# Moving an adaptation vector from vector, Pool and scalar work to column-tiled matmuls, in a hybrid decoder layer on one Trainium2 core

## The chip, the core and the metric

The program runs on one NeuronCore of one Trainium2 chip. TensorE (PE) does the matmuls, and its loading of the stationary operand is shown apart as PEld. VectorE (DVE), ScalarE (ACT) and GpSimd (POOL) do the elementwise work, and SyncE (SP) issues nearly all DMAs. The metric is the time of one execution on the device in microseconds (us). All data are float32; the large matmuls split each operand into a rounded part (hi) and a rest (lo) and add three products in the faster fp32r form.

## The reference

One decoder layer on x (1024 tokens, 1024 channels), conditioned on a vector c of 1024 numbers. What matters here is the first line: `mod` has 6 x 1024 entries, and each of its six parts shifts, scales or gates the whole layer.

```python
c_act = jax.nn.silu(c)
mod = (c_act @ w_ada[l] + b_ada[l])[:, None, :]          # 1024 x 6144 weights, 25 MB
shift1, scale1, gate1, shift2, scale2, gate2 = jnp.split(mod, 6, axis=-1)
h = rms_norm(x, norm1_w[l]) * (1.0 + scale1) + shift1
proj = h @ w_in[l]                    # split into DeltaNet heads (gq gk gv gz ga gb) and attention (sq sk sv)
...                                   # conv + silu + l2 norm, chunked delta rule; sliding-window attention
x = x + gate1 * (jnp.concatenate([o_g, o_s], axis=-1) @ w_out[l])
h2 = rms_norm(x, norm2_w[l]) * (1.0 + scale2) + shift2
x = x + gate2 * ((jax.nn.silu(h2 @ w_gate[l]) * (h2 @ w_up[l])) @ w_down[l])
```

## The kernel before

Activations lie transposed: channels on the 128 partitions, tokens along the free axis, in two halves of 512 tokens. Channel tile k (0 to 7) of x and of h holds channels 128k to 128k+127. The vector `mod` is kept in `modc`, 128 x 48: column u holds entries 128u to 128u+127. Columns 0 to 7 are shift1, 8 to 15 scale1, 16 to 23 gate1, 24 to 31 shift2, 32 to 39 scale2, 40 to 47 gate2. Each column ("unit" u) needs 512 KB of weights, loaded by one DMA (`load_ada`) into a tile `ada{u}`. These tiles share slots by tags: two slots each for b, c, d and e, and other tiles (halves of x, `kd`, `bv`) use the same slots earlier or later.

In the kernel before, row n of unit u's tile is output channel 128u+n, with 1024 weights. silu(c) is spread over all partitions once (`cb`), and a unit is one product with `cb` and a sum along the row. `mod_col` and `start_col` do this in one DVE instruction (CUSTOM_DVE, 128x1024) and a short read of the accumulator, or in a POOL product and an ACT copy with a sum; a DVE addition puts the bias on.

The program has these stages up to the attention scan:

- Start. The sums of squares of the first half of x go through `rstd`; then, tile by tile, `start_in(k)` makes the scale a (from unit 8+k) and the shift sh (from unit k), and from them the modulated h, hi by ACT and lo by DVE (`start_lo`). As soon as tile k is there, `start_mm` multiplies it with the weights of the first units gk0, gk1, gq0, gq1 and with those of three token blocks of the small unit skv. `JOIN` says after which tile a unit begins. The function `o` fixes the order of DVE, ACT and POOL here.
- Second half: `norm1_gen(1)`, then `modulate1` for the eight tiles of the second half of x.
- Fill: a loop of `ADA_ITER` = 14 rounds. Each round issues six steps (`fill(6)`) of the stream of dense matmuls on PE and works off two of the units 16 to 43.
- Token scalars and pairs: `token_gen` makes decay and beta (matmuls `psg`, then `pst`), and the four head pairs go through statistics (`pst_k`, `pst_q`), scaling (`psr_k`) and products (`psA`), with fills of fixed length between (`VISITS_A`).
- Solve: DVE solves the triangular systems (`soltmp`, `lanes`), while value and query visits and the last four units (44 to 47) run beside it (`VISITS_B`). Then the chunk scan begins, at about 345 us.

PE runs in the order in which the code is written. On DVE, ACT, POOL and SP a scheduler fixes one order per engine when the program is built. Each engine works strictly in its own order.

Of the kernel before, what the change touches and what calls it, by code (L numbers as in the profile page):

```python
# [8 lines left out]
F32 = mybir.dt.float32  # L9
# [3 lines left out]
AF = mybir.ActivationFunctionType  # L13
ALU = mybir.AluOpType
# [3 lines left out]
P = 128  # L18
T = 1024
TH = 512  # L20
D = 1024
KT = D // P
# [5 lines left out]
ADA_TAGS = "bcd" * 5 + "bcde" * 4 + "d"  # L28
ADA_ITER = 14
# [25 lines left out]
def tile_hybrid_layer(  # L55
# [175 lines left out]
    a1 = cp.tile([P, KT], F32, name="a1")  # L231
    a2 = cp.tile([P, KT], F32, name="a2")
    adat = {}

    act.activation(out=c_col, in_=c_col, func=AF.Silu)
    cb = t4("cb")
    ps_c = [sm(f"ps_c{g}") for g in range(2)]
    for i in range(KT):
        pe.transpose(out=ps_c[i // 4][:, i % 4 * P:(i % 4 + 1) * P], in_=bc(c_col[:, i:i + 1], (P, P)), identity=ident)

    def copy_cb():
        for g in range(2):
            act.activation(out=cb[:, half(g)], in_=ps_c[g], func=AF.Copy)

    def load_ada(u, tag=None):
        adat[u] = t4(f"ada{u}", tag=tag)
        done["ada"] = sp.dma_start(out=adat[u], in_=ada[u])

    def mod_col(u, eng=dve, bias=True):

        w = adat.pop(u)
        if eng is dve:
            dve.tensor_tensor_reduce(out=w, in0=w, in1=cb, scale=1.0, scalar=0.0, op0=ALU.mult, op1=ALU.add,
                                     accum_out=modc[:, u:u + 1])
        else:
            eng.tensor_tensor(out=w, in0=w, in1=cb, op=ALU.mult)
            act.activation(out=w, in_=w, func=AF.Copy, accum_out=modc[:, u:u + 1])
        if bias:
            dve.tensor_tensor(out=modc[:, u:u + 1], in0=modc[:, u:u + 1], in1=b_ada[:, u:u + 1], op=ALU.add)

    ada_next = [16]

    def ada_some(n, tag, eng=dve):
        for u in range(ada_next[0], ada_next[0] + n):
            if "kd" in done:
                with tc.issue_after(done["kd"].ins):
                    load_ada(u, tag)
            else:
                load_ada(u, tag)
            mod_col(u, eng)  # L270
        ada_next[0] += n


    def rstd(ps, name):
# [170 lines left out]
    def start_col(u):  # L445
        w = adat.pop(u)
        o(dve, "tensor_tensor_reduce", out=w, in0=w, in1=cb, scale=1.0, scalar=0.0, op0=ALU.mult, op1=ALU.add,
          accum_out=modc[:, u:u + 1])

    def start_split(hi, lo, src):  # L450
        o(act, "activation", out=r(hi), in_=src, func=AF.Copy)
# [25 lines left out]
    for k in range(KT):  # L477
        if k % 2 == 0:
            pair = t4(f"sq{k}_0", (P, 2, TH))
        sqk[k] = pair[:, k % 2]  # L480
        o(act, "activation", out=sqk[k], in_=xs(k, 0), func=AF.Square)
        if k == 5:
            for g in range(2):
                o(act, "activation", out=cb[:, half(g)], in_=ps_c[g], func=AF.Copy)
# [24 lines left out]
    start_col(0)  # L509
    with tc.issue_after(queue[dve].ins):  # L510
        rs = rstd(ps, "n1_0")
    queue[dve] = rstd_done["n1_0"]
# [8 lines left out]

    ps_u = [bank(t, f"ps_{kind}{p}_0") for t, (kind, p) in zip(("u", "sw", "u", "sw"), START)]
    ps_s = [sm(f"ps_skv{i}", i) for i in range(3)]

    def start_mm(u, k):
        if u < 4:
            mm3(ps_u[u], wpart(wg[u], k), h_hl(0)(k), k == 0, k == KT - 1)
        else:
            for i in range(3):
                skv_mm(ps_s[i], i, k)  # L530

    def start_in(k):

        a, sh, x = a1[:, k:k + 1], modc[:, k:k + 1], xs(k, 0)
        hi = h_hl(0)(k)[0]
        if k:
            start_col(k)
            start_lo(k - 1)
        start_col(8 + k)
        o(dve, "scalar_tensor_tensor", out=a, in0=modc[:, 8 + k:9 + k], scalar=n1w[:, k:k + 1],  # L540
          in1=pre1[:, k:k + 1], op0=ALU.mult, op1=ALU.add)
        o(dve, "tensor_tensor", out=sh, in0=sh, in1=b_ada[:, k:k + 1], op=ALU.add)
        if k in START_DVE:
            o(dve, "scalar_tensor_tensor", out=x, in0=x, scalar=a, in1=rows[0], op0=ALU.mult, op1=ALU.mult)
            o(act, "activation", out=r(hi), in_=x, func=AF.Identity, bias=sh)
        else:
            o(act, "activation", out=r(hi), in_=x, func=AF.Identity, scale=a, bias=sh)
            o(act, "activation", out=x, in_=x, func=AF.Identity, scale=a, bias=sh)

    def start_lo(k):  # L550
        hi, lo = h_hl(0)(k)
        x = xs(k, 0)
        if k in START_DVE:
            o(dve, "scalar_tensor_tensor", out=r(lo), in0=x, scalar=modc[:, k:k + 1], in1=hi, op0=ALU.add, op1=ALU.subtract)
        else:
            o(dve, "tensor_tensor", out=r(lo), in0=x, in1=hi, op=ALU.subtract)
# [3 lines left out]
    for k in range(KT + 1):  # L560
        if k < KT:
            if k + 2 < KT:
                for u in LOADS[k + 1]:
                    load_w(u)
                load_pair(k + 2)
            start_in(k)
            for step in POOL_AT[k]:
                if step[0] == "w":
                    start_split(wg[step[1]][0], wg[step[1]][1], w_raw[step[1]])
                elif step[0] == "m":  # L570
                    o(pool, "tensor_tensor", out=xs(step[1], 0), in0=xs(step[1], 0), in1=rows[0], op=ALU.mult)
                else:
                    ks_ = slice(2 * step[1], 2 * step[1] + 2)
                    start_split(wk_hi[:, ks_], wk_lo[:, ks_], wk_raw[:, ks_])
        else:
            start_lo(k - 1)
            n1 = norm1_gen(1, 3)
            next(n1)
            ktok = t4("ktok", (P, NB, P))
            vs = t4("vs", (P, NB, P))  # L580
        if k:
            for u in have:
                start_mm(u, k - 1)
            if k <= 2:
                keep_warm(WARM[2 + k])
# [299 lines left out]
    def fill(n):  # L885
        with tc.high_priority():
            for _ in range(n):
                next(dense, None)

    def val(p):  # L890
        run(value_gen(p))

    for i in range(ADA_ITER):
        fill(VISITS_A[0])
        with tc.issue_after(h_done[0].ins), tc.issue_after(h_done[1].ins):
            ada_some(1, ADA_TAGS[2 * i], pool if i not in ADA_DVE else dve)
            ada_some(1, ADA_TAGS[2 * i + 1])
    next(token)
    p0, p1, p2, p3 = PAIRS
    for n, visit in zip(VISITS_A[1:], (token, token, p2, p0, p2, p0, p2, p1, p0, keys, p1, p3, keys, p1, keys, p3, p3)):  # L900
# [45 lines left out]
    for n, visit in zip(VISITS_B, (v0, v1, v2, v3, q0, q0, q1, q1, q2)):  # L946
        fill(n)
        next(visit)
        if visit is v3:
            for i in range(32 - 2 * ADA_ITER):  # L950
                ada_some(1, "b", pool if i % 4 else dve)
    dve.scalar_tensor_tensor(out=a2, in0=modc[:, 32:40], scalar=1.0, in1=n2w, op0=ALU.add, op1=ALU.mult)


# [699 lines left out]
```

## Time and profile before

| | before |
|---|---|
| median of 3 runs | 1319.22 us (1318.56 to 1321.34) |
| profiled execution, own time | 1316.65 us |
| its span on the core | 1314.9 us |
| PE busy | 1192.7 us (91%) |
| DVE busy | 892.6 us (68%) |
| POOL busy | 629.4 us (48%) |
| ACT busy | 538.8 us (41%) |

The span is the time between the first and the last recorded instruction; the rest of the execution's own time lies around it. The shares are means over all stages, and the stages differ: what is changed lies nearly all in the first 345 us, where DVE is the busiest engine, while from there on PE is nearly always busy. Idle time of an engine costs something only where the end waits for it. Fp32 matmuls other than transposes stand as two records each in the trace.

### The profile page before, as it was taken

How to read it: one execution, taken by the hardware profiler on the slowest of the kernel's cores; microseconds unless marked ns; L12 is line 12 of the kernel's file. 1: busy time of each engine (PE TensorE's matmuls, PEld its weight loads, DVE VectorE, ACT ScalarE, POOL GpSimd, SP SyncE). 2: the span in 40 equal slices, each digit the busy share in tenths (PEclk: the TensorE clock that was granted, in tenths of full speed). 3: DMA queues.
4: the chain of work that ended last, by engine and by line, in shares of the span. 5: the costliest groups of instructions: out<-in, count | busy, mean ns of one | idle time of the engine just before them, and what ended most of it. 6: DMA issues, size and time to landing. Idle time of an engine off the chain costs nothing.

```text
span 1314.9 us, 18979 instructions
## 1 busy us (share of the span) xinstructions
PE 1192.7 (91%) x6710; PEld 974.5 (74%) x6710; DVE 892.6 (68%) x1690; ACT 538.8 (41%) x1028; POOL 629.4 (48%) x453
## 2 busy tenths in 40 slices
PE   6867697896999799997998999999999999999998
PEld 5757576684788678785786788777777888888887
DVE  7999989979724677576646416877876875546430
ACT  4373555422434777434356432222232334544430
POOL 4667344534335444344354455545455545455440
PEclk8899799898999899998899999999999999999999
DMA  8727468485639865366845625556665567775651
GB/s 326 233 85 273 144 132 227 133 229 183 199 126 205 132 113 165 106 218 216 288 157 187 207 95 203 208 200 228 212 212 201 176 217 281 250 252 195 201 168 40
DMA packets 167214, 250.62 MB, mean 191 GB/s; under 512 B 40656, under 2 KB 106448, under 8 KB 165584
## 3 DMA queue, kind: packets, MB, share of 16 engines
q1 hardware_dynamic: 157520, 241.03, 56.6%
q0 software_dynamic: 9600, 8.39, 3.9%
q8 instruction: 53, 0.87, 0.3%
q14 instruction: 41, 0.34, 0.1%
HBM read 182.89 MB, written 66.45 MB: 190 GB/s over the span
## 4 chain that ended last, share of the span: by engine, by line
PE 43%; DVE 16%; DMA 8%; issue 4%; POOL 3%; ACT 3%; SPq 0%; DVEq 0%; ACTq 0%; POOLq 0%
PE ps_P L1359 5%; PE ps_P L1358 5%; PE ps_P L1360 5%; DMA wb<-in_wgate_dram 4%; PE ps_S L1358 2%; PE ps_S L1359 2%; PE ps_S L1360 2%; PE ps_c L1358 2%; PE ps_c L1359 2%; POOL wS L193 2%; PE ps_c L1360 2%; DVE wa L1427 1%; PE ps_gz L212 1%; DMA SD<-sd 1%; DVE soltmp L817 1%
## 5 line engine op out<-in xcount | busy, mean ns | idle before, releaser
L193 POOL TENSOR_TENSOR wP<-rP,wP 128x512 fp32r<-128x512 f32 (+1 forms) x84 | 108.3, 1301 | 105.3 <-ACT wP L192 100.2
L1359 PE MATMUL ps_P<-t,wP 128*128 128x512 f32 x308 | 120.4, 391 | 0.0
L1358 PE MATMUL ps_P<-t,wP 128*128 128x512 f32 x308 | 120.4, 391 | 0.0
L1360 PE MATMUL ps_P<-t,wP 128*128 128x512 f32 x308 | 120.2, 390 | 0.0
L193 POOL TENSOR_TENSOR wS<-wa,wS 128x512 fp32r<-128x512 f32 x44 | 62.8, 1437 | 111.8 <-ACT wS L192 78.9
L1360 PE MATMUL ps_S<-T,wS 128*128 128x512 f32 x264 | 102.8, 390 | 0.3 <-POOL wS L193 0.3
L1359 PE MATMUL ps_S<-T,wS 128*128 128x512 f32 x264 | 102.9, 390 | 0.0
L1358 PE MATMUL ps_S<-T,wS 128*128 128x512 f32 x264 | 102.9, 390 | 0.0
L192 ACT ACTIVATE wP<-rP 128x512 fp32r<-128x512 f32 (+1 forms) x84 | 48.4, 590 | 77.6 <-PE ps_P L1360 49.2
L1358 PE MATMUL ps_c<-B,w 128*128 128x512 f32 x176 | 70.5, 401 | 6.1 <-ACT X L1398 6.1
L1360 PE MATMUL ps_c<-B,w 128*128 128x512 f32 x176 | 69.7, 396 | 0.0
L1359 PE MATMUL ps_c<-B,w 128*128 128x512 f32 x176 | 69.7, 396 | 0.0
L1465 ACT ACTIVATE sg<-sg 128x512 f32<-128x512 f32 x33 | 20.9, 632 | 116.0 <-DVE sg L1461 116.0
L1358 PEld LDWEIGHTS ps_P<-t,wP 128*128 128x128 f32 x308 | 57.9, 188 | 12.6
L1360 PEld LDWEIGHTS ps_P<-t,wP 128*128 128x128 f32 x308 | 57.9, 188 | 12.5
L1359 PEld LDWEIGHTS ps_P<-t,wP 128*128 128x128 f32 x308 | 57.8, 188 | 12.4
L192 ACT ACTIVATE wS<-wa 128x512 fp32r<-128x512 f32 x44 | 26.7, 624 | 94.6 <-DVE wa L1426 71.8
L1424 DVE TENSOR_TENSOR ws<-wb 128x512 f32<-128x512 f32 x22 | 23.1, 1051 | 62.1 <-DMA wb<-in_wgate_dram 54.5
L1360 PEld LDWEIGHTS ps_S<-T,wS 128*128 128x128 f32 x264 | 49.6, 188 | 11.1 <-POOL wS L193 0.7
L212 PE MATMUL ps_o<-mix,w_o 128*128 128x512 f32 x128 | 53.7, 420 | 4.2 <-ACT w_o L192 4.2
L1358 PEld LDWEIGHTS ps_S<-T,wS 128*128 128x128 f32 x264 | 49.6, 188 | 10.5
L1359 PEld LDWEIGHTS ps_S<-T,wS 128*128 128x128 f32 x264 | 49.6, 188 | 10.5
(507 smaller groups left out, 3559.4 us busy)
## 6 DMA issues: line engine op xcount, KB each, us to landing
ada<-in_ada_dram SPq DMA_DIRECT2D x48, 512.0 KB, 4.7
AD<-ops SPq DMA_DIRECT2D x11, 1536.0 KB, 5.0
rP<-SD SPq DMA_DIRECT2D x16, 704.0 KB, 5.7
sd<-in_wdown_dram SPq DMA_DIRECT2D x20, 512.0 KB, 5.3
SD<-sd SPq DMA_DIRECT2D x20, 512.0 KB, 3.9
rP<-in_wdown_dram SPq DMA_DIRECT2D x12, 704.0 KB, 5.3
XD<-X SPq DMA_DIRECT2D x22, 256.0 KB, 3.3
xu<-XD SPq DMA_DIRECT2D x22, 256.0 KB, 3.4
```

The source lines that it names most:

```text
L192: act.activation(out=r(hi), in_=src, func=AF.Copy)
L193: last = eng.tensor_tensor(out=r(lo), in0=src, in1=hi, op=ALU.subtract)
L212: pe.matmul(out, lhsT=r(lhs[0]), rhs=r(rhs[0]), start=first, stop=False)
L817: dve.tensor_tensor(out=tv[g], in0=bc(L[:, i, i + 1:32].unsqueeze(1), (P, i, 31 - i)), in1=bc(L[:, 0:i, i:i + 1], (P, i, 31 - i)), op=ALU. ...
L1358: pe.matmul(ps, lhsT=r(wh), rhs=r(xh), start=first and i == 0, stop=False, **kw)
L1359: pe.matmul(ps, lhsT=r(wh), rhs=r(xl), start=False, stop=False, **kw)
L1360: pe.matmul(ps, lhsT=r(wl), rhs=r(xh), start=False, stop=i == n - 1, **kw)
L1424: dve.tensor_tensor(out=s1, in0=a21, in1=a22, op=ALU.add)
L1427: dve.tensor_tensor(out=a12, in0=a12, in1=a11, op=ALU.subtract)
L1465: act.activation(out=out, in_=out, func=AF.Silu)
```

## The change

The weights of a unit are stored the other way (tile `[p, k, n]`: input channel 128k+p, output channel n), with as many bytes. For each unit PE now does eight matmuls in plain fp32 (`ada_rows`): stationary is column k of silu(c), repeated over 32 columns, moving are the 128x128 weights of k. Matmul k goes to column group k mod 4 of the array and so to PSUM partitions 32g to 32g+31. The four partial sums then lie as rows. ACT copies them to SBUF, and one matmul per unit with `sel` (ones at partitions 0, 32, 64, 96) sums them and turns them into a column (`ada_cols`). A DVE addition adds the bias, for four units at a time in the fill and solve stages (`ada_gen`). The DVE, POOL and ACT instructions of `mod_col` and `start_col` are gone, with `cb` and its eight transposes, and the last two blocks of warm-up transposes. In the start stage the columns of tile k stand on PE behind the products of tile k-1. In the fill stage the rows of a group stand after every second round, its copy and its columns one and two groups later, and four more dense steps run before `token`.

```diff
-    def mod_col(u, eng=dve, bias=True):
-        w = adat.pop(u)
-        if eng is dve:
-            dve.tensor_tensor_reduce(out=w, in0=w, in1=cb, scale=1.0, scalar=0.0, op0=ALU.mult, op1=ALU.add,
-                                     accum_out=modc[:, u:u + 1])
-        else:
-            eng.tensor_tensor(out=w, in0=w, in1=cb, op=ALU.mult)
-            act.activation(out=w, in_=w, func=AF.Copy, accum_out=modc[:, u:u + 1])
...
+    def ada_rows(out, us):
+        for n, u in enumerate(us):
+            w = adat.pop(u)
+            for k in range(KT):
+                g = k % 4
+                pe.matmul(out[32 * g:32 * g + 32, n * P:(n + 1) * P], lhsT=bc(c_col[:, k:k + 1], (P, 32)), rhs=w[:, k],
+                          start=k < 4, stop=k >= 4, tile_position=(0, 32 * g))
+
+    def ada_cols(out, row, n):
+        for i in range(n):
+            pe.matmul(out[:, i:i + 1], lhsT=row[:, i * P:(i + 1) * P], rhs=sel, start=True, stop=True)
...
+    def ada_gen(us, q=None):
+        ps = sm(f"ps_ada{us[0]}", q)
+        ada_rows(ps, us)
+        yield
+        row, n = t2(f"ada_row{us[0]}"), len(us)
+        act.activation(out=row[:, 0:n * P], in_=ps[:, 0:n * P], func=AF.Copy)
+        yield
+        ada_cols(ps, row, n)
+        u = us[0]
+        dve.tensor_tensor(out=modc[:, u:u + n], in0=ps[:, 0:n], in1=b_ada[:, u:u + n], op=ALU.add)
+        yield
...
+            start_rows(k)
+        if k:
+            start_lo(k - 1)
+            for u in have:
+                start_mm(u, k - 1)
+        if k < KT:
+            start_cols(k)
             start_in(k)
...
     for i in range(ADA_ITER):
         fill(VISITS_A[0])
         with tc.issue_after(h_done[0].ins), tc.issue_after(h_done[1].ins):
-            ada_some(1, ADA_TAGS[2 * i], pool if i not in ADA_DVE else dve)
-            ada_some(1, ADA_TAGS[2 * i + 1])
+            ada_load(1, ADA_TAGS[2 * i])
+            ada_load(1, ADA_TAGS[2 * i + 1])
+        if i % 2:
+            for g in gens:
+                next(g, None)
+            gens = [g for g in (gens + [ada_gen(ada_open[-4:])])][-3:]
+            next(gens[-1])
+    for _ in range(2):
+        fill(2)
+        for g in gens:
+            next(g, None)
     next(token)
```

What that does to the order on PE in the start stage, around tile 1: before, the products of tile 1 (units gk0 and gk1) follow straight on those of tile 0, and those of gq0 follow on them.

```order
L212 MATMUL ps_gk0_0_297<-h0_130,w_s0_141 128x512
L213 MATMUL ps_gk0_0_297<-h0_130,w_s0_141 128x512
L214 MATMUL ps_gk0_0_297<-h0_130,w_s0_141 128x512
L212 MATMUL ps_gk1_0_298<-h0_130,w_s1_143 128x512
L213 MATMUL ps_gk1_0_298<-h0_130,w_s1_143 128x512
L214 MATMUL ps_gk1_0_298<-h0_130,w_s1_143 128x512
L212 MATMUL ps_gq0_0_299<-h0_130,w_s2_145 128x512
```

Now the same products (numbers of lines and buffers have shifted) have the rows of tile 2 (units 2 and 10) ahead of them and the columns of tile 2 behind them:

```order
L251 MATMUL ps_ada_296<-ada2_298,sml_99 32x128 x8
L251 MATMUL ps_ada_296<-ada10_300,sml_99 32x128 x8
L212 MATMUL ps_gk0_0_289<-h0_125,w_s0_136 128x512
L213 MATMUL ps_gk0_0_289<-h0_125,w_s0_136 128x512
L214 MATMUL ps_gk0_0_289<-h0_125,w_s0_136 128x512
L212 MATMUL ps_gk1_0_290<-h0_125,w_s1_138 128x512
L213 MATMUL ps_gk1_0_290<-h0_125,w_s1_138 128x512
L214 MATMUL ps_gk1_0_290<-h0_125,w_s1_138 128x512
L257 MATMUL ps_ada_296<-sel_119,ada_row0_318 128x1 x2
L212 MATMUL ps_gq0_0_291<-h0_125,w_s2_140 128x512
```

The columns of tile 2, which everything for tile 2 waits for, now stand behind the products of tile 1.

Second place, PE in the fill stage, in the dense unit gq2 of the first half. Before, it runs without a break:

```order
L213 MATMUL ps_gq2_0_804<-h0_130,w_gq2_641 128x512
L214 MATMUL ps_gq2_0_804<-h0_130,w_gq2_641 128x512
L212 MATMUL ps_gq2_0_804<-h1_131,w_gq2_641 128x512
L213 MATMUL ps_gq2_0_804<-h1_131,w_gq2_641 128x512
L214 MATMUL ps_gq2_0_804<-h1_131,w_gq2_641 128x512
```

Now the first group's rows (units 16 to 19) stand in it, six matmuls from its beginning:

```order
L213 MATMUL ps_gq2_0_920<-h0_125,w_gq2_762 128x512
L214 MATMUL ps_gq2_0_920<-h0_125,w_gq2_762 128x512
L251 MATMUL ps_ada16_931<-ada16_897,sml_99 32x128 x8
L251 MATMUL ps_ada16_931<-ada17_899,sml_99 32x128 x8
L251 MATMUL ps_ada16_931<-ada18_927,sml_99 32x128 x8
L251 MATMUL ps_ada16_931<-ada19_929,sml_99 32x128 x8
L212 MATMUL ps_gq2_0_920<-h1_126,w_gq2_762 128x512
L213 MATMUL ps_gq2_0_920<-h1_126,w_gq2_762 128x512
```

All later PE work stands behind unit 18's rows, and these need the DMA of unit 18. Third place, SP, where these loads stand. Before:

```order
L247 DMA ada20_846<-in_ada_dram 128x1024
L247 DMA ada19_816<-in_ada_dram 128x1024
L204 DMA w_gk0_1r_1107<-in_wmain_dram 128x1024
L204 DMA w_gq0_1r_1154<-in_wmain_dram 128x1024
L204 DMA w_gk1_1r_1202<-in_wmain_dram 128x1024
L247 DMA ada22_874<-in_ada_dram 128x1024
L247 DMA ada18_811<-in_ada_dram 128x1024
```

And now:

```order
L243 DMA ada20_990<-in_ada_dram 128x1024
L243 DMA ada19_929<-in_ada_dram 128x1024
L204 DMA w_gq0_1r_1443<-in_wmain_dram 128x1024
L204 DMA w_gk1_1r_1486<-in_wmain_dram 128x1024
L243 DMA ada22_1013<-in_ada_dram 128x1024
L243 DMA ada23_1015<-in_ada_dram 128x1024
L243 DMA ada18_927<-in_ada_dram 128x1024
```

Unit 18's load stands late on SP in both. It has tag d, and both d slots hold the last four channel tiles of the second half of x until `modulate1` is through with them.

## Rows read from the trace of the kernel before

**Rows 1.** Windows by stage: stretch, then busy us of each engine, granted clock.
```profile
0.00:71.20 71.20, 53.78 (x272) 45.46 (x273) 58.67 (x87) 31.34 (x51) 38.92 (x42) 0.86 0.77 268
...
98.60:159.20 60.60, 41.73 (x213) 36.04 (x213) 60.16 (x113) 26.25 (x53) 35.12 (x14) 0.87 0.64 226
159.20:276.90 117.70, 101.52 (x673) 83.39 (x672) 103.44 (x185) 56.49 (x85) 55.20 (x25) 0.92 0.63 165
276.90:345.00 68.10, 52.34 (x248) 43.07 (x246) 63.46 (x179) 17.50 (x28) 26.94 (x19) 0.90 0.60 178
```

**Rows 2.** Groups by line and shape, DVE, 0 to 345 us: busy us, mean ns.
```profile
L438 DVE CUSTOM_DVE_ANT_0 ada<-ada,cb 128x1024 f32<-128x1024 f32 x16 | 27.2, 1700 | 0.5 <-DMA ada<-in_ada_dram 0.5
L253 DVE CUSTOM_DVE_ANT_0 ada<-ada,cb 128x1024 f32<-128x1024 f32 x15 | 20.4, 1361 | 0.0
...
L259 DVE TENSOR_TENSOR modc<-modc,sml 128x1 f32<-128x1 f32 x32 | 9.6, 314 | 0.1
...
L332 DVE SCALAR_TENSOR_TENSOR h<-xt,modc,h 128x512 fp32r<-128x512 f32 x4 | 7.1, 1786 | 0.0
L330 DVE SCALAR_TENSOR_TENSOR xt<-xt,a,row_n 128x512 f32<-128x512 f32 x4 | 6.5, 1690 | 1.4 <-ACT row_n L288 1.4
...
L438 DVE SCALAR_TENSOR_TENSOR h<-xt,modc,h 128x512 fp32r<-128x512 f32 x4 | 6.0, 1512 | 0.1
```

**Rows 3.** Groups by line and shape, POOL, 0 to 345 us.
```profile
L256 POOL TENSOR_TENSOR ada<-ada,cb 128x1024 f32<-128x1024 f32 x17 | 42.6, 2518 | 29.7 <-DMA ada<-in_ada_dram 13.4 <-DVE soltmp L817 10.4 <-DVE modc L259 5.7
```

**Rows 4.** Timelines of DVE and ACT: start us, us; one tile's h, then the second half.
```profile
57.87 0.82 ACT L438 ACTIVATE h<-xt,modc,a 128x512 fp32r<-128x512 f32 x1 [1.76 <-DVE modc L438]
...
92.61 0.74 DVE L332 SCALAR_TENSOR_TENSOR h<-xt,modc,h 128x512 fp32r<-128x512 f32 x1
...
97.37 1.28 DVE L337 TENSOR_TENSOR h<-xt,h 128x512 fp32r<-128x512 f32 x2
```

**Rows 5.** Timeline of PE: warm-up, end of the start stage, dense matmuls, psg.
```profile
17.73 3.83 PE L304 MATMUL warm<-ident 128*128 128x128 f32 x32
...
71.22 0.95 PE L321 MATMUL ssps<-ones,sq 128*128 128x1 f32 x8
...
104.16 0.39 PE L213 MATMUL ps_gq<-h,w_gq 128*128 128x512 f32 x1
104.38 0.39 PE L214 MATMUL ps_gq<-h,w_gq 128*128 128x512 f32 x1
...
110.00 0.29 PE L214 MATMUL ps_skv<-wk_hi,h 128*128 128x272 f32 x1
110.13 0.29 PE L212 MATMUL ps_skv<-wk_hi,h 128*128 128x272 f32 x1
...
157.73 0.69 PE L666 MATMUL psg<-tsc,tribd 128*128 128x64 f32 x2 [12.11 <-DVE tsc L661]
```

**Rows 6.** Timeline of PE: small and full fp32 matmuls (stationary size, moving size, records).
```profile
197.40 2.59 PE L781 MATMUL psA<-kq,kn 64*64 64x128 f32 x64
...
362.48 1.16 PE L1039 MATMUL pk<-S,kvq 128*128 128x128 f32 x8
363.39 0.48 PE L212 MATMUL ps_gz<-h,w_gz 128*128 128x512 f32 x1
...
388.99 0.68 PE L1054 MATMUL pd<-rvt,kvq 64*64 64x64 f32 x16
389.51 1.09 PE L1064 MATMUL po<-rvt,aqb 64*64 64x64 f32 x16
```

**Rows 7.** DMA issues, 0 to 100 us: count, KB each, us to landing.
```profile
ada<-in_ada_dram SPq DMA_DIRECT2D x25, 512.0 KB, 4.6
```

**Rows 8.** Timeline of DVE and POOL in the solve.
```profile
311.58 5.00 POOL L256 TENSOR_TENSOR ada<-ada,cb 128x1024 f32<-128x1024 f32 x2 [10.41 <-DVE soltmp L817]
...
314.25 2.59 DVE L817 TENSOR_TENSOR soltmp<-lanes 128x238 f32<-128x238 f32 x1
319.06 0.38 DVE L817 TENSOR_TENSOR soltmp<-lanes 128x228 f32<-128x228 f32 x1
```

More of the change, by code (lines that the diff above doesn't have):

```diff
@@ L235, in tile_hybrid_layer, with ada_load @@
     act.activation(out=c_col, in_=c_col, func=AF.Silu)
[L236 to L243, printed above, removed]
+    sel = cp.tile([P, 1], F32, name="sel")
+    pool.memset(sel, 0.0)
+    for g in range(4):
+        pool.memset(sel[32 * g:32 * g + 1], 1.0)
     def load_ada(u, tag=None):
-        adat[u] = t4(f"ada{u}", tag=tag)
+        adat[u] = t4(f"ada{u}", (P, KT, P), tag=tag)
         done["ada"] = sp.dma_start(out=adat[u], in_=ada[u])
-    def mod_col(u, eng=dve, bias=True):
-        w = adat.pop(u)
-        if eng is dve:
-            dve.tensor_tensor_reduce(out=w, in0=w, in1=cb, scale=1.0, scalar=0.0, op0=ALU.mult, op1=ALU.add,
-                                     accum_out=modc[:, u:u + 1])
-        else:
-            eng.tensor_tensor(out=w, in0=w, in1=cb, op=ALU.mult)
-            act.activation(out=w, in_=w, func=AF.Copy, accum_out=modc[:, u:u + 1])
-        if bias:
-            dve.tensor_tensor(out=modc[:, u:u + 1], in0=modc[:, u:u + 1], in1=b_ada[:, u:u + 1], op=ALU.add)
+    def ada_rows(out, us):
[8 more added lines that the diff above has]
+            pe.matmul(out[:, i:i + 1], lhsT=row[:, i * P:(i + 1) * P], rhs=sel, start=True, stop=True)
     ada_next = [16]
-    def ada_some(n, tag, eng=dve):
+    ada_open = []
+    def ada_load(n, tag):
         for u in range(ada_next[0], ada_next[0] + n):
@@ L269, in ada_some @@
                 load_ada(u, tag)
-            mod_col(u, eng)
+            ada_open.append(u)
         ada_next[0] += n
+    def ada_gen(us, q=None):
[9 more added lines that the diff above has]
+        yield
     def rstd(ps, name):
@@ L443, in load_pair, with start_rows, start_cols @@
             load_ada(u, tag)
[L445 to L448, printed above, removed]
+    adarow = {}
+    def start_rows(k):
+        ada_rows(ps_a[:, k % 2 * 256:], (k, k + 8))
+    def start_cols(k):
+        if not k:
+            adarow[0] = t2("ada_row0")
+        row = adarow[0][:, k % 2 * 256:k % 2 * 256 + 256]
+        o(act, "activation", out=row, in_=ps_a[:, k % 2 * 256:k % 2 * 256 + 256], func=AF.Copy)
+        ada_cols(ps_a[:, k % 2 * 256:], row, 2)
     def start_split(hi, lo, src):
@@ L481, in tile_hybrid_layer @@
         o(act, "activation", out=sqk[k], in_=xs(k, 0), func=AF.Square)
-        if k == 5:
-            for g in range(2):
-                o(act, "activation", out=cb[:, half(g)], in_=ps_c[g], func=AF.Copy)
         if k:
@@ L508, in tile_hybrid_layer @@
         pe.matmul(ps[:, i:i + 1], lhsT=sqk[0][:, i * P:(i + 1) * P], rhs=ones1, start=True, stop=True)
-    start_col(0)
     with tc.issue_after(queue[dve].ins):
@@ L523, in tile_hybrid_layer @@
     ps_s = [sm(f"ps_skv{i}", i) for i in range(3)]
+    ps_a = sm("ps_ada", 3)
     def start_mm(u, k):
@@ L535, in start_in @@
         hi = h_hl(0)(k)[0]
[L536 to L540, printed above, removed]
+        pa = ps_a[:, k % 2 * 256:]
+        o(dve, "scalar_tensor_tensor", out=a, in0=pa[:, 1:2], scalar=n1w[:, k:k + 1],
           in1=pre1[:, k:k + 1], op0=ALU.mult, op1=ALU.add)
-        o(dve, "tensor_tensor", out=sh, in0=sh, in1=b_ada[:, k:k + 1], op=ALU.add)
+        o(dve, "tensor_tensor", out=sh, in0=pa[:, 0:1], in1=b_ada[:, k:k + 1], op=ALU.add)
         if k in START_DVE:
@@ L575, in tile_hybrid_layer @@
         else:
-            start_lo(k - 1)
             n1 = norm1_gen(1, 3)
@@ L581, in tile_hybrid_layer @@
         if k:
[L582 to L585, printed above, removed]
             for new in [u for u in range(5) if JOIN[u] == k - 1]:
@@ L891, in val @@
         run(value_gen(p))
+    gens = []
     for i in range(ADA_ITER):
@@ L949, in tile_hybrid_layer @@
         if visit is v3:
-            for i in range(32 - 2 * ADA_ITER):
-                ada_some(1, "b", pool if i % 4 else dve)
+            ada_load(32 - 2 * ADA_ITER, "b")
+            gens = ada_gen(ada_open[-4:], 2)
+        if visit in (q0, q1):
+            next(gens, None)
     dve.scalar_tensor_tensor(out=a2, in0=modc[:, 32:40], scalar=1.0, in1=n2w, op0=ALU.add, op1=ALU.mult)
@@ L1632 @@
         "rowvec": _np.concatenate([f["a_log"][0], f["dt_bias"][0], f["sinks"][0]]),
-        "ada": w_ada.T.reshape(48, P, D),
+        "ada": tiles(w_ada),
         "wmain": tiles(_np.concatenate([w_in[:, 512:1024], w_in[:, 0:512], w_in[:, 1024:2048], w_in[:, 2064:2576]], axis=1)),
```

## Prediction, written before the changed kernel ran

> **What bounds it now.** I read the windows by stage first. In the start stage DVE is busy for 58.7 of 71.2 us and PE for 53.8; in the fill stage (98.6 to 159.2 us) DVE for 60.2 of 60.6 and PE for 41.7; between the token scalars and the last pair product (159.2 to 276.9) DVE for 103.4 of 117.7 and PE for 101.5; in the solve DVE for 63.5 of 68.1 [rows 1]. So DVE leads in each, though in the third stretch PE is close behind. The groups by line then say how much of DVE's time belongs to the vector: 27.2 us of products in the start, 20.4 in fill and solve, and 32 additions with 9.6 us [rows 2]; POOL spends 42.6 us in 17 products [rows 3]. The timeline shows where PE feels it: `psg` waits 12.11 us for DVE's `tsc` and starts at 157.73 [rows 5]. After 345 us PE hardly waits, and a time won or lost earlier shifts the rest.
>
> The removed instructions are thus on the busiest engine. What speaks against a plain gain is that in the start and the fill PE now does the vector itself, in its own strict order, and waits for its DMAs there.
>
> **Price of a unit on PE.** Eight plain fp32 matmuls stand as 16 records with a 128-column moving side. No row of before has 32 stationary columns in four column groups. Two rows bound the price. `psA`, 64x64 in alternating quarters of the array with 128 columns moving: 2.59 us for 64 records, 40 ns each. `pk`, the full array with 128 columns: from 362.48 to 363.39 for 8 records, 114 ns each [rows 6]. I take the former, as only there do neighbours in the program use different parts of the array: 16 x 40 = 0.65 us per unit. At 114 ns it is 1.82 us. The columns of four units are 8 records, priced like the 8 of `ssps`, 0.95 us [rows 5].
>
> One thing speaks against the low price. `psA` alternates in rows and columns of the array; the new matmuls use all rows. `pd` and `po`, both with one half of the rows, stand at 0.68 and 1.09 us for 16 records [rows 6]: `pd` alternates between column halves and `po` does not, so columns alone do overlap. The Trainium skill ("TensorE: Matmul & The Clock Gate", Part 3: Packing small matmuls) says that a weight load overlaps running matmuls only if its row group differs. By that rule the four column groups run one after the other, and the sum would take 1.82 us for a unit in place of 0.65; the `pd` row speaks for overlap.
>
> **(a) Start stage, +7 us (2 to 12).** DVE loses 27.2 us of products. But PE's order now ties tile k to tile k-1: the columns of k stand behind all products of k-1. From these columns to the end of the products of k the chain is: columns of two units 0.48, then `a` and `sh` on DVE 0.3 to 0.6, h on ACT 0.82 and x as long [rows 4], `lo` on DVE 0.74 (by the undisturbed `L332` of the same size [rows 4]), and the products. One dense matmul follows another after 0.22 us and one with 272 columns after 0.13 [rows 5], so 12 and 9 of them take 3.85 us, of which 3.6 lie behind `lo`. That is about 7.0 us per tile, with PE idle for half of it. A walk with these steps from the end of the shortened warm-up (17.73 + 24 x 0.12 = 20.6 [rows 5]) and the units joining as before gives columns at 31.4 (tile 2), 42.7 (tile 4), 52.9 (tile 5), 59.9 and 66.9, and the last product at 73.1, against 71.2 now [rows 1, 5]. This holds no disturbance. h on DVE takes 1512 ns in the mean here [rows 2], about double of 0.74, with POOL splitting weights beside it; that stays, is now inside the chain, and ACT has the second half's loads and copies before some of the h. I add 5 us for it: +7, between the floor of 2 and 12 with twice that.
>
> **(b) Second half, -4 us (-8 to 0).** Here POOL's products are gone. `L332` and `L330` average 1786 and 1690 ns [rows 2] where an undisturbed one takes 0.74 [rows 4]: 8 x 1.0 = 8 us of excess. POOL also has other work, so I take half.
>
> **(c) Fill, `psg` 17.7 us later.** Unit 18's tile has tag d and waits until `modulate1` ends, 98.65 us before (97.37 + 1.28 [rows 4]), then 4.6 us for its DMA [rows 7]. All later PE work stands behind that wait. From there to `psg` PE has, by the order, 144 dense matmuls of 512 columns (x 0.2275 = 32.8), 96 of 272 (x 0.125 = 12.0), 26 units' rows (x 0.65 = 16.9) and seven sets of columns (x 0.95 = 6.7): 68.2 us, and about 1 for the slower clock after the wait. So `psg` starts at 98.6 + 7 - 4 + 4.6 + 68.2 + 1 = 175.4, and not at 157.7. DVE falls to some 40 us of work here and is no longer the bound: of its gain of 20 us nothing can be used. Among these 68.2 us are the rows and columns, 23.6 us, which PE did not have; before, it idled 18.9 us here [rows 1]. That is the crux: work is moved into the one engine that cannot be late afterwards. With 114 ns per record the 26 units take 47.3 in place of 16.9: +30.4. With 32 ns, pd's spacing to `po` (0.52 / 16 [rows 6]), -3.4.
>
> **(d) To the last `psA`, -3 us (-14 to 0).** Four more dense steps (12 matmuls, 2.7 us) and one DVE convolution of about that size now lie ahead of `psg` and no longer in this stretch. No adaptation work lay between 159.2 and 276.9, so DVE's 103.4 us [rows 1] stay otherwise; PE's 101.5 stay less 2.7. The idle 16.2 us of PE could at the most be given back if the later `psg` finds DVE's queue already worked off, hence the far end.
>
> **(e) Solve, -4 us (-7.4 to 0).** `soltmp` takes 2.59 us while POOL runs a product of two (5.00 us) and 0.38 otherwise [rows 8]. Three such cases and one product of 1.36 on DVE [rows 2] make 7.4. Against it stands that the last group's four units share the two slots of tag b, so the third and fourth wait for the first's rows on PE and then for a DMA of 4.6 us [rows 7], with PE standing still: I take 4.
>
> **(f) From the scan on, -2.7 us (-2.7 to 0).** The dense work done earlier is missing here, where PE is the bound.
>
> **Sum.** +17.7 (a, b and c together) - 3 - 4 - 2.7 = +8.0. The profiled execution has 1316.65 us, so 1324.7; the median of the runs shown lies 2.6 above it, and the same offset gives **1327 us**. Edits costed at nothing are the bias additions (one per four units, in DVE's idle time), the ACT copies (ACT is busy for 35 of 61 us at the most in the fill [rows 1]) and the `sel` memsets before the first load has landed.
>
> **Rivals.** What a measurement of this kernel can tell from no change is about 0.2%, 2.6 us.
>
> *Faster, 1315 (chance 0.25).* The place is the stretch behind `psg`. PE's idle 16.2 us there are waits for DVE's statistics and scalings. In the fill DVE now has 20 us of idle time, and by its order takes up what the scheduler puts there: second-half convolutions and the solve's preparation. If 12 us more than I assume are worked off ahead of `psg`, the stretch shrinks by (d)'s far end and the sum is +8.0 - 12 = -4.0, that is 1315 for the median; with (a) at its floor 1310. It decides from about 8 us worked off. For it speaks DVE's 88% share in the stretch; against it, that the pairs' work depends on q and k that PE makes late.
>
> *The column groups run serially, 1362 (0.13).* Then 30.4 us are added in the fill and about 5 in the start (two units' rows, 2.3 us more per tile, partly in PE's idle time): 1327 + 35. The Trainium skill's rule, weighed above, would give this; `pd` against `po` speaks against it.
>
> *The terms cancel, within 2.6 us of 1319 (0.12).* The start at its floor (-5) and the solve at its far end (-3.4) are enough.
>
> **How the numbers follow.** My forecast, slower by 3 to 20 us, has 0.50; serial columns 0.13; faster 0.25; none 0.12. So faster 0.25, same 0.12, slower 0.63. For the range I leave one in ten out on each side: 1310 below (the faster case with little beyond its middle) and 1352 above, which is short of full serial running but holds a price of about 85 ns per record or a start at +12 with more waits for loads. The forecast's own range is 1322 to 1339.
>
> **What the profile after would show.** Rows of four units in 2.6 us of PE (7.3 if serial). The last product of the start near 78 us, with PE idle for 3 us ahead of each tile's first products, released by ACT or DVE. A PE wait for the DMA of unit 18 near 102 to 106, and `psg` near 175 with no wait for DVE. `L332` and `L330` near 1.2 us. DVE half idle in the fill, but as long as before, 100 us or more, between `psg` and the last `psA`, which ends near 290. `soltmp` at 0.4 us throughout, and a PE wait for the DMA of unit 46. Wrong it would be above all if `psg` came at 165 or earlier, or if the stretch behind it took 105 us or less.

## The result, and the profile after

The changed kernel is slower: 1359.51 us in the median of 4 runs (1350.97 to 1361.23) against 1318.89 before, ratio 1.028 [1.023, 1.033]. The forecast was 1327, with a range that ended at 1352. The profiled execution has 1360.69 us, 44.0 more than that of before. Where the lead is lost is read from the PE timelines, at four places that both programs pass:

| start of, us | before | after | later by | forecast |
|---|---|---|---|---|
| `ssps` behind the last product of the start | 71.22 | 84.53 | 13.3 | 7 |
| `psg` | 157.73 | 178.09 | 20.4 | 17.7 |
| last `psA` | 271.94 | 302.48 | 30.5 | 14.7 |
| first `psm` (scan) | 353.85 | 389.49 | 35.6 | 10.7 |
| end of the span | 1314.9 | 1358.7 | 43.8 | 8.0 |

The lines of the last `psA` and the first `psm`, before and after:

```profile
271.94 2.59 PE L781 MATMUL psA<-kq,kn 64*64 64x128 f32 x64
353.85 1.09 PE L997 MATMUL psm<-tx,aqb 32*32 32x32 f32 x32
...
302.48 2.59 PE L797 MATMUL psA<-kq,kn 64*64 64x128 f32 x64 [2.28 <-DVE kq L781]
389.49 1.09 PE L1025 MATMUL psm<-tx,aqb 32*32 32x32 f32 x32
```

The windows by stage of the changed kernel (stretch, its length, busy us of PE, PEld, DVE, ACT and POOL with counts, granted clock, DMA share, GB/s) answer to [rows 1]:

```profile
0.00:84.50 84.50, 64.50 (x544) 54.70 (x545) 27.20 (x55) 33.60 (x53) 32.94 (x47) 0.90 0.67 232
84.50:108.20 23.70, 12.67 (x100) 10.70 (x98) 21.99 (x41) 15.24 (x33) 9.43 (x6) 0.90 0.28 89
108.20:178.10 69.90, 66.92 (x713) 58.54 (x714) 25.31 (x62) 19.78 (x40) 7.18 (x3) 0.94 0.53 189
178.10:305.10 127.00, 100.49 (x664) 82.12 (x662) 102.47 (x180) 58.69 (x86) 53.79 (x24) 0.88 0.57 149
305.10:390.00 84.90, 69.71 (x397) 56.24 (x398) 62.56 (x189) 19.72 (x31) 28.65 (x20) 0.90 0.65 188
```

DVE falls from 58.7 to 27.2 us in the start and to 25.3 of 69.9 in the fill, where PE has 66.9. Behind `psg` DVE has as much to do as before, 102.5 us, in a stretch that grew. The timeline of the changed kernel (start, us, engine; wait in brackets) shows the places at which PE stands:

```profile
56.78 0.50 PE L257 MATMUL ps_ada<-sel,ada_row 128*128 128x1 f32 x4
58.73 0.49 PE L212 MATMUL ps_gk<-h,w_s 128*128 128x512 f32 x1
...
60.42 1.06 ACT L192 ACTIVATE w_gk2h<-w_gk2r 128x1024 fp32r<-128x1024 f32 x1 [1.85 <-DMA w_gk2r<-in_wmain_dram]
61.39 0.80 ACT L451 ACTIVATE xt<-xt,modc,a 128x512 f32<-128x512 f32 x1
...
61.56 2.35 POOL L193 TENSOR_TENSOR w_gk2l<-w_gk2r,w_gk2h 128x1024 fp32r<-128x1024 f32 x1 [4.88 <-ACT w_gk2h L192]
...
62.22 2.23 DVE L451 TENSOR_TENSOR h<-xt,h 128x512 fp32r<-128x512 f32 x1 [4.55 <-ACT xt L451]
...
64.51 0.80 PE L213 MATMUL ps_gk<-h,w_s 128*128 128x512 f32 x1 [5.28 <-DVE h L451]
70.40 0.50 PE L257 MATMUL ps_ada<-sel,ada_row 128*128 128x1 f32 x4
...
98.24 1.08 PE L251 MATMUL ps_ada<-ada,sml 128*32 128x128 f32 x32
111.17 1.94 PE L251 MATMUL ps_ada<-ada,sml 128*32 128x128 f32 x32 [11.86 <-DMA ada<-in_ada_dram]
...
123.21 1.95 PE L251 MATMUL ps_ada<-ada,sml 128*32 128x128 f32 x64
125.09 0.50 PE L212 MATMUL ps_gk<-h,w_gk2h 128*128 128x512 f32 x1
...
178.09 0.33 PE L682 MATMUL psg<-tsc,tribd 128*128 128x64 f32 x2
...
210.85 1.97 PE L741 MATMUL psr_k<-ident,wide_k 128*128 128x128 f32 x8 [8.46 <-ACT wide_k L737]
...
345.72 1.08 PE L251 MATMUL ps_ada<-ada,sml 128*32 128x128 f32 x16 [7.75 <-DMA ada<-in_ada_dram]
```

Four units' rows take 125.09 - 123.21 = 1.88 us for 64 records: 29.4 ns each, 0.47 us a unit. In the start, ACT's split of a weight tile, itself waiting for its load, stands between h and x of one tile, and POOL's half of the split runs into `lo`, so PE waits 5.28 us. In the fill PE waits 11.86 us for unit 18. In the solve it waits for units 44 to 47, 11.4 us in all, and 7.75 us of that for unit 45. The waits of PE up to 390 us (us in total, times, longest):

```profile
PE ps_ada L251 <- DMA ada<-in_ada_dram: 23.3, 5, 11.9
PE psr_k L741 <- ACT wide_k L737: 13.2, 2, 8.5
```

### The profile page after: what moved, and what is told of

Its sections match the earlier page's. It is cut to its first block, busy times and chain, and to the rows that moved or that the text cites. A ratio compares the mean times of both kernels' runs of the same rounds, so it can differ in the third digit from the quotient of the medians.

```text
span 1358.7 us, 20582 instructions
## 1 busy us (share of the span) xinstructions
PE 1234.5 (91%) x7558; PEld 1011.6 (74%) x7558; DVE 817.3 (60%) x1604; ACT 529.0 (39%) x1010; POOL 581.5 (43%) x441
## 4 chain that ended last, share of the span: by engine, by line
PE 54%; DVE 20%; DMA 12%; issue 5%; ACT 4%; POOL 3%; SPq 1%; DVEq 0%; ACTq 0%; POOLq 0%
PE ps_P L1386 5%; PE ps_P L1388 5%; PE ps_P L1387 5%; DMA wb<-in_wgate_dram 3%; PE ps_S L1386 2%; PE ps_S L1388 2%; PE ps_c L1386 2%; PE ps_S L1387 2%; PE ps_c L1387 2%; PE ps_c L1388 2%; DMA SD<-sd 2%; POOL wS L193 2%; DMA sd<-in_wdown_dram 2%; PE ps_ada L251 1%; DVE wa L1455 1%
## 5 line engine op out<-in xcount | busy, mean ns | idle before, releaser
L1452 DVE TENSOR_TENSOR ws<-wb 128x512 f32<-128x512 f32 x22 | 26.4, 1198 | 60.0 <-DMA wb<-in_wgate_dram 55.7
```

The source lines that it names most:

```text
L1452: dve.tensor_tensor(out=s1, in0=a21, in1=a22, op=ALU.add)
```

## The experiments

The theory formed from these rows is one of waits: PE's strict order puts the columns of a tile too late, and units 18 and 45 to 47 are asked for before their slots are free. The rival is one of work: the loss is simply the matmuls that PE did not have before (48 x 0.47 us of rows and some 11 us of columns, about 34 us). All edits are to the changed kernel where nothing else is said.

**First group off tag d.**

```diff
-ADA_TAGS = "bcd" * 5 + "bcde" * 4 + "d"
+ADA_TAGS = "bcbc" + "ddbc" + "bcdd" + "bcde" * 4
```

> Units 16 to 19 take the tags b, c, b, c in place of b, c, d, b, so none of the first group needs a slot that the second half of x still holds; the two d slots go to units 20 and 21. Theory of the waits: the 11.86 us that PE stood before the rows of unit 18 go, psg comes at 167 to 170 in place of 178, and the time falls by 8 to 11 us, to about 1350. Rival, the work itself: the loss is the 34 us of matmuls that PE did not have before, PE has little else to do while it waits, and the time falls by less than 3 us.

Measured: 1.0185 [1.0146, 1.0225] of before. `psg` comes at 169.36 though the start ended 1.5 us later, and the longest wait for a load there is 1.2 us. The ratio fell by about 13 us, a little more than expected. So the wait was paid in full.

**Columns earlier in the start.**

```diff
-            for u in have:
+            for u in have[:1]:
                 start_mm(u, k - 1)
...
             start_cols(k)
             start_in(k)
+        for u in have[1:]:
+            start_mm(u, k - 1)
```

> In the start stage the columns of tile k and its scale, shift and h stand behind the products of tile k-1 with the first unit only, and ahead of those with the other units. Theory of the order: the chain of a tile runs beside three of four or five products, the last product ends at 74 to 78 us in place of 84.5, and the time falls by 6 to 10 us. Rival: the start is held by its loads and by the weight splits on ACT and POOL, the end of the stage moves by less than 3 us and so does the time.

Measured: 1.0176 [1.0143, 1.0208]; the start ends at 76.27, and the ratio fell by about 14 us, more than expected. Later kernels with this start, in the same order on PE, DVE and ACT, ended it at 71.53, 79.86 and 76.06, so it differs by 8 us between executions, more than with the start as it was changed (84.5 to 87.1 in seven profiles). The two ranges do not meet.

**The last four units as two pairs.**

```diff
-            gens = ada_gen(ada_open[-4:], 2)
+            steps = [lambda: ada_rows(ps_l, us[:2]), lambda: ada_rows(ps_l[:, 256:], us[2:]), last_copy, last_cols]
```

> The last four units run as two pairs: the rows of 44 and 45 at the first visit of the first query, those of 46 and 47 sixteen dense steps later, then one copy and the columns. Theory of the waits: of the 11.4 us of waits for these units' loads some 8 stay out, and the time falls by 5 to 9 us. Rival: the chain to wide_s, for which the kernel before waited 13.4 us at the same place, is next; the first psm moves by less than 2 us and so does the time.

Measured: 1.0264 [1.0223, 1.0304]. The waits for units 46 and 47 are gone, but that for unit 45 is not:

```profile
341.00 1.08 PE L251 MATMUL ps_last<-ada,sml 128*32 128x128 f32 x16 [7.29 <-DMA ada<-in_ada_dram]
356.19 1.08 PE L251 MATMUL ps_last<-ada,sml 128*32 128x128 f32 x32
```

The last `psA` to the first `psm` takes 82.3 us in place of 87.0 (81.9 before), so the place is right in part. The wait for unit 45, 6.7 to 8.0 us, stays in every later kernel with two last pairs; no run here removes it. The scan behind it was 12 us longer in this profile, and the time hardly moved, against the 5 to 9 us expected. More on that below.

**Half of the rows.**

```diff
-            for k in range(KT):
+            for k in range(4):
...
-                          start=k < 4, stop=k >= 4, tile_position=(0, 32 * g))
+                          start=True, stop=True, tile_position=(0, 32 * g))
```

> Only the matmuls with the first four of the eight input tiles are done for each unit, one per column group, so each entry is a sum over half of its inputs. All loads, slots, copies, columns and waits stay. Rows take half, about 0.24 us per unit in place of 0.47. If the loss is PE's added work, the time falls by all of it, 11 us. By the theory of the waits only the 26 units behind the wait for unit 18 count, and it falls by 5 to 7 us.

Measured: 1.0232 [1.0183, 1.0282], some 7 us less, though the interval overlaps that of the changed kernel. The trace is clearer: `psg` comes at 170.90, 7.2 earlier, with the start 0.7 us longer. So of PE's work that of the fill is paid, as the theory of the waits has it, and not all 11 us.

**All three edits.**

> The three edits together: first group off tag d, columns of tile k ahead of most products of tile k-1, last four units as two pairs. If the parts add, the start ends at 76 us, psg comes at 159 to 161, the last psA at 281 to 284 and the first psm at 362 to 366 (353.85 in the kernel before), and the ratio to the kernel before is 1.006 to 1.012. Rival: the parts share one cause (whatever PE gains early it waits for later), and the ratio stays above 1.014.

Measured: 1.0135 [1.0109, 1.0161], a little above the expected range and just below the rival's 1.014. `psg` comes at 154.84, 3 us ahead of the kernel before. Then the lead is lost: last `psA` at 277.73, first `psm` at 362.60. So a loss sits behind `psg` that none of the three edits touches.

**Without the extra dense steps.**

```diff
-    for _ in range(2):
-        fill(2)
-        for g in gens:
-            next(g, None)
     next(token)
...
         fill(n)
+        for g in gens:
+            next(g, None)
```

> As the run with all three edits, but without the four extra dense steps ahead of psg: the last two groups' copies and columns go with the first two visits of the token scalars. Theory: the extra steps bring one more convolution to DVE and ACT, which the order puts into the chain from psg to the first scaling, and take four steps of cover from later. Then psg to the last psA falls from some 122 us to 114 to 117, as in the kernel before, and the ratio to before is 1.000 to 1.006. Rival: these stretches are long for another reason; psg comes 3 us earlier, psg to the last psA stays at 121 or more, and the time is that of the run with all three edits.

Measured: 1.0093 [1.0062, 1.0123], above the expected range. `psg` to the first `psr_k` falls from 32.8 to 26.9 us (27.7 before), but to the second from 41.5 only to 40.6 (35.8 before), and `psg` to the last `psA` is 119.5 (122.9 with the steps). Half of the theory held.

**One column group.** All eight matmuls at tile position (0, 0), adding up in one row.

> The changed kernel with all eight matmuls of a unit in column group 0, adding up in one row; only that row is copied and turned. If the four column groups run beside each other, as the 29.5 ns per record say, then one group costs 58 ns (the po row) to 114 ns (the pk row) per record, 0.93 to 1.8 us per unit, and the time rises by 12 to 35 us over the changed kernel. Rival, the rule that loads overlap only across row groups: the four groups did not run beside each other either, the price per unit stays at 0.47 us, and so does the time.

Measured: 1.067 [1.0635, 1.0705], 1408.31 us, 49 more than the changed kernel and above the 12 to 35 expected. The timeline of PE has four units in 7.17 us, 112 ns a record:

```profile
149.88 7.17 PE L250 MATMUL ps_ada<-ada,sml 128*32 128x128 f32 x64
```

So the four column groups do run beside each other, 3.8 times as fast. That one group also adds up in one row is not what makes it slow: the products of `pk` [rows 6] go to columns of their own and take 114 ns.

**The start of before, fill on PE.** Units 0 to 15 as in the kernel before, 16 to 47 on PE, first group off tag d, two last pairs, no extra steps.

> The start stage of the kernel before (its products on DVE, cb, order and warm-up), but units 16 to 47 on PE as in the changed kernel, with the first group off tag d, the last four as two pairs and no extra dense steps. If the loss lies in the start's order, in the waits for unit 18 and for units 45 to 47 and in the extra steps, all four are gone: the start ends at 71 to 73, psg comes at 152 to 155 (157.73 before), and the ratio is 0.995 to 0.999. Rival: PE's added work of the fill is paid in full behind psg, the stretch to the last psA is 121 us or more as in the changed kernel, and the ratio is 1.003 or more.

Measured: 1.0062 [1.0038, 1.0086]; `psg` at 149.10, but 120.4 us to the last `psA` (114.2 before). The ratio is the rival's and the stretch nearly so: of the lead of 8.6 us, 6.2 were given back there. DVE's groups say with what, and it is not PE's work. In the kernel before, DVE did three convolution steps on keys between `psg` and the first `psA`; here and in the changed kernel it does nine, and ACT loads its function tables more often. Groups of the kernel before, 157.7 to 197.4 us (busy us, mean ns):

```profile
L365 DVE SCALAR_TENSOR_TENSOR kn<-ps_gk,sml,kn 128x511 f32<-128x511 f32 (+2 forms) x3 | 2.2, 746 | 2.9 <-ACT kn L363 2.9
...
L379 ACT ACT_TABLE_LOAD x1 | 1.3, 1283 | 3.4 <-DVE kn L371 3.4
```

and of the changed kernel, 178.1 to 223.5 us:

```profile
L378 DVE SCALAR_TENSOR_TENSOR kn<-ps_gk,sml,kn 128x511 f32<-128x511 f32 (+2 forms) x9 | 6.7, 740 | 2.0 <-ACT kn L376 2.0
...
L392 ACT ACT_TABLE_LOAD x3 | 3.8, 1283 | 3.4 <-DVE kn L384 3.3
```

The six more belong to pair 3. Its tile `kn3` is one of six in a pool of 4 KB slots. In the program before, `cb` kept one of the six to the end of the solve, and `kn3` had to wait for pair 2's tile. The change takes `cb` away, `kn3` gets its place at once, and the fixed orders of DVE and ACT now put its convolution ahead of the scalings that PE waits for.

**The slot kept.** A tile like `cb` is read once, when the first values are there:

```diff
+    hold = t4("hold")
+    pool.memset(hold[:, 0:1], 0.0)
...
+    pool.tensor_tensor(out=held, in0=hold[:, 0:1], in1=vts[0][:, 0:1], op=ALU.add)
```

> The changed kernel with one more tile that keeps a slot of the 4 KB pool until the value visits, as cb did in the kernel before. Theory of the freed slot: without cb, pair 3's keys (kn3) get a slot at once, and their nine convolution steps and the ACT table loads stand on DVE and ACT ahead of the scaling of pairs 2 and 0, for which PE waits. With the slot kept, kn3 has to wait for pair 2's tile again, psg to the first psA falls from 45.4 us to 39 to 41, and the time by 4 to 7 us. Rival: the four extra dense steps alone make that stretch long; it stays at 44 or more, and the time within 2 us of the changed kernel.

Measured: `psg` to the first `psA` is 41.1 us (45.4 without), but the time is 1.030 [1.0256, 1.0342], no better, where 4 to 7 us were expected: the scan took 202.4 us in place of 187.6. In the first 41 us DVE now has three key steps and ACT one of these table loads:

```profile
L381 DVE SCALAR_TENSOR_TENSOR kn<-ps_gk,sml,kn 128x511 f32<-128x511 f32 (+2 forms) x3 | 2.2, 742 | 2.0 <-ACT kn L379 2.0
...
L395 ACT ACT_TABLE_LOAD x1 | 1.3, 1283 | 0.0
```

> All three edits, no extra dense steps, and the slot kept. By the theory psg to the first psA falls from 46.0 us to 39 to 41, the first psm comes at 355 to 358 (353.85 before), and the ratio to before is 1.003 to 1.007 (1.0093 without the kept slot). Rival: it is lost again at the next wait, and the ratio stays at 1.009.

Measured: 1.0017 [0.9993, 1.0042]; `psg` to the first `psA` 38.9 us (46.0 without the slot), first `psm` at 351.01, earlier than expected. That is no difference from the kernel before.

> The start of the kernel before, fill and last four units on PE, no extra dense steps, and cb's slot kept until the value visits. By the theory psg comes at 149 again, psg to the first psA takes 39 to 41 us in place of 46.4, and the first psm is at 345 to 348, 6 to 9 us ahead of the kernel before: ratio 0.995 to 1.002. Rival: the stretches behind psg give the lead back whatever kn3 does, and the ratio is that of the same kernel without the kept slot, 1.006.

Measured: 0.9968 [0.9946, 0.999]; 39.1 us (46.4 without), first `psm` at 345.61. So the freed slot is shown as a cause three times. Up to the last `psA` the three pairs agree better still: `psg` to there is 116.9, 112.3 and 112.5 us with the slot kept, 124.4, 119.5 and 120.4 without, so the slot is worth 7.2 to 7.9 us.

**Half of the fill on PE.** As the last, with units 16, 17, 20, 21, ... on PE, 18, 19, 22, 23, ... on DVE, none on POOL.

> As the last one, but in the fill only two of each four units go to PE and two stay on DVE; none goes to POOL. PE then has 14 units' rows and fewer columns less, some 9 us, and DVE 14 products of 1.2 us that POOL no longer disturbs. By the theory of PE as the bound of the fill, psg comes at 140 to 145 and the ratio is 0.990 to 0.997. Rival: with the DVE products back, psg waits for DVE's tsc as in the kernel before, psg stays at 149 or later, and the ratio is 0.998 or more.

Measured: 0.9917 [0.9879, 0.9955], 1312.37 us: faster than both kernels, by 0.8% against the one before. Its windows:

```profile
71.10:95.00 23.90, 20.12 (x129) 16.53 (x128) 22.19 (x43) 16.34 (x33) 11.39 (x6) 0.97 0.39 119
95.00:140.90 45.90, 45.90 (x417) 39.95 (x416) 37.83 (x96) 15.39 (x35) 6.40 (x3) 0.98 0.70 271
140.90:257.90 117.00, 98.73 (x669) 81.29 (x668) 102.19 (x189) 57.04 (x85) 53.92 (x26) 0.91 0.64 165
```

In the fill PE is now busy all of 45.9 us and DVE for 37.8: with the work shared, `psg` comes at 140.91, 10.1 us ahead of the run before it. Of the 17.2 us by which the first `psm` is earlier than in the kernel before (336.62 for 353.85), the time keeps about 11.

**The scan, again.** Gains up to the first `psm` did not always reach the end. Further executions of the kernel before and of two edited ones ask whether the scan behind it is the kernel's or the execution's doing.

> The kernel before, unchanged, profiled again. From the first psm to the last one it took 186.1 us. If the length of the chunk scan is a matter of the clock granted in one execution and not of the kernel, this profile shows another length, between 186 and 202 us, with the same waits. Rival: the scan of the kernel before always takes 186 us, and the edits make it longer.

> As the last one, a further execution: between 186 and 202 us from the first psm to the last by the theory of the execution, 186 again by the rival.

> The changed kernel with the last four units as two pairs, profiled again. Its first profile had 199.7 us from the first psm to the last, at a granted clock of 0.5 to 0.8 in several stretches of 10 us. By the theory of the execution another length, 187 to 202 us, while the first psm stays within 2 us of 381. Rival: the edit itself makes the scan longer, and it takes 198 us or more again.

> The changed kernel with the slot kept, profiled again: first profile 202.4 us from the first psm to the last. By the theory of the execution 187 to 202 us, and psg to the first psA again 41 us. Rival: keeping the slot makes the scan longer, 200 us or more again.

Windows from the first `psm` to the last, of the kernel before in the second of its three profiles:

```profile
353.49:547.90 194.41, 185.42 (x1808) 151.88 (x1808) 108.80 (x429) 110.34 (x296) 78.03 (x82) 0.91 0.64 144
```

of the kernel with the last four units as two pairs:

```profile
382.74:582.50 199.76, 189.75 (x1795) 155.38 (x1794) 102.46 (x430) 110.31 (x296) 76.42 (x81) 0.87 0.61 137
```

and of the changed kernel:

```profile
389.49:577.12 187.63, 177.63 (x1796) 145.64 (x1795) 105.36 (x436) 110.53 (x296) 76.90 (x82) 0.94 0.65 146
```

The kernel before took 186.1, 194.4 and 191.4 us in three profiles, with its first `psm` within 0.5 us each time: 8 us belong to the execution, and the granted clock goes with it (0.98, 0.91, 0.94). That speaks against the rival. But the kernel with two last pairs took 199.6 and 199.8, and that with the kept slot 202.4 and 200.3 (0.87 and 0.88), twice alike. That speaks against the theory, and the kernel with all three edits had 197.7 at 0.88. So within one kernel the lower clock goes with the longer scan; across kernels it does not tell all (187.6 to 193.9 us at 0.94), and what sets it in a kernel stays open. From the first `psm` to the end the kernel before took 961.1, 970.9 and 966.2 us, the changed kernel 969.2.

## Why the prediction was wrong

**What bounds the kernel, (b) and (c)** held. DVE was freed, and the second half fell from 27.4 to 23.7 us (-3.7; forecast -4). Taking half of the excess was right for a reason that the rows show: of the two slow DVE steps, `L330` and `L332` of before (`L343` and `L345` now), only one had POOL's products beside it (two groups of DVE, busy us and mean ns, then the timeline of POOL).

```profile
L343 DVE SCALAR_TENSOR_TENSOR xt<-xt,a,row_n 128x512 f32<-128x512 f32 x4 | 7.0, 1808 | 1.4 <-ACT row_n L301 1.4
...
L345 DVE SCALAR_TENSOR_TENSOR h<-xt,modc,h 128x512 fp32r<-128x512 f32 x4 | 2.9, 737 | 0.0
...
91.45 6.41 POOL L347 TENSOR_TENSOR xt<-xt,row_n 128x512 f32<-128x512 f32 x4 [3.94 <-ACT row_n L301]
```

`L345` fell from 1786 to 737 ns, while `L343` still has POOL's own four tiles beside it and stays at 1808 (1690 before). The fill is PE's: from unit 18 to `psg` 66.9 us, forecast 68.2 and 1 for the clock, which was granted at 0.50 for 4.8 us behind the wait. The load landed 3.0 us behind the last row of `modulate1`, not 4.6. That `psg` came within 3 us of the forecast is partly luck: the start was 6 us longer than forecast, the fill 4 us shorter, and in the fill cheaper units (12.2 us in place of 16.9) made up for other work that was 3.4 us dearer.

**The price of a unit** was taken too high, 0.65 us for 0.47: the alternating column groups need 29.4 ns per record, near the 32 of `pd` and not the 40 of `psA` [rows 6]. The rival of serial groups named 1362 us, nearly the measured time, and was nevertheless wrong: serial groups cost what the run with one group shows, 112 ns, as the `pk` row said, and 1408 us. The Trainium skill ("TensorE: Matmul & The Clock Gate", Part 3: Packing small matmuls) says that a weight load overlaps running matmuls only where the row group differs. The trace does not agree: these matmuls share all rows, and at 29.4 against 112 ns they do run beside each other. The same section of the Trainium skill has a measured gain of 2.38 for three column tiles. The 3.8 for four goes the same way.

**(a), the start, was mis-sized**: 13.3 us in place of 7, just outside its range of 2 to 12. The walk has the columns of tiles 5, 6 and 7 at 52.9, 59.9 and 66.9; they came at 56.78, 70.40 and 77.58. So more than half of the 11 us over the walk arose at one place, where a weight split in ACT's order, waiting for its load, kept PE from the products of tile 5 for 5.28 us. The waits ahead of the other tiles were 0.3 to 1.9 us, not the 3 expected everywhere. The allowance of 5 us for disturbance should have been 11. With the columns moved forward the stage ends 8 us sooner, as it must if the order is the cause.

**(d) is the step that failed**: "DVE's 103.4 us stay otherwise", -3 (-14 to 0). The work did stay (102.5), but its order did not: the stretch from `psg` to the last `psA` grew by 10.2 us. Two things did it. The slot that `cb` no longer holds let `kn3` in ahead of the scalings; keeping it takes 7.5 us off the stretch in the changed kernel. The extra dense steps brought a convolution into the chain to the first scaling; leaving them out takes off 3.4 us (122.9 to 119.5). At the first scaling the two overlap: `psg` to the first `psr_k` is 32.8 us with both, 26.9 without the steps and 24.1 with the slot kept. With both undone, and the other edits in, the stretch takes 112.3 us (114.2 before). The range ended at 0, so a longer stretch had no place in the forecast. The forecast costed `cb` as a removed copy and never as a freed place.

**(e), the solve, has the wrong sign**: -4 forecast, +5.1 measured. DVE did gain: no `soltmp` takes over 0.4 us any more (the gain by the prediction's own rows is 3 x 2.21 + 1.36 = 8.0, not 7.4). But the waits for the last units were 11.4 us, where the forecast left 3.4 for them, and it named the third and fourth unit where the longest wait is for the second, unit 45: its load stands on SP behind one that waits 4.7 us for the values, and is issued only at 339.58 us (wait in total, times, longest; then the timeline of SP).

```profile
SPq L1053 <- DMA BV<-bv: 4.7, 1, 4.7
...
338.73 0.80 SPq L1053 DMA_DIRECT2D kvq<-BV  x2
339.58 7.61 SPq L243 DMA_DIRECT2D ada<-in_ada_dram  x3
```

With the waits for 46 and 47 gone the stretch still takes 82.3 us (81.9 before), so DVE's gain was not used; what it would give without the wait for unit 45 is not shown. **(f) and the rest** were forecast at -2.7 and are +8.2: 1.5 in the scan, 3.8 from there to the first `ps_S`, and some 3 behind. Since the kernel before itself took 961 to 971 us from the first `psm` to its end, and the changed one 969, I do not put this part down to the change. Whether the 2.7 us came back here cannot be told within that spread.

So the loss up to the first `psm` is told: 13.3 in the start, -3.7 in the second half, 10.8 more up to `psg` by the wait for unit 18 and the rows on PE, 10.2 in the pairs, 5.1 in the solve. Of the 36 us by which the forecast of 8.0 was short of the 43.8 measured, 3 arose up to `psg`, 13 in (d), 9 in (e) and 11 from the scan on. It is both theories: the larger part are waits (the edits that only move work or keep a slot take the ratio from 1.028 to 1.002), the smaller is work on PE, which the fill pays (`psg` 7.2 us earlier with half of the rows).

## What to carry to other kernels

Before work is moved to the engine with the strictest order, ask for each moved step what it must wait for there and who queues behind it: here PE stood 17 us for one load and one weight split, half of what all the added matmuls take (about 34 us). A removed tile is also a freed slot, and where a scheduler fixes the orders, something else will move into its place and perhaps into a chain. And work that overloads one engine is shared rather than moved: half of the fill's units on PE and half on DVE, with none on POOL, beat both. What all of them on DVE with none on POOL would give was not run.

## What was not expected of the hardware

Four plain fp32 matmuls that use all 128 rows and one column group each run 3.8 times as fast as four in the same group (29.4 against 112 ns per record). The granted clock of TensorE in one and the same scan, with the same instructions up to it, was 0.98, 0.91 and 0.94 in three executions, and the scan took 186, 194 and 191 us. The falls come where the last dense unit is through and PE has only the scan's small matmuls. In the second of these executions no dense matmul runs from 417 to 507 us; the clock is 1.00 up to 423.5 and 0.57 in the 10 us after that, though PE is busy for 9.0 of them. In the changed kernel it is 0.50, the lower of its two levels (1.2 GHz), from 459.5 to 469.5 us, in a like place.
